# A float32 product with block-diagonal weights, issued as four 64x64 tiles in place of two 128x128 products

## The chip, the cores and the metric

The kernel runs on one core of a Trainium2 chip. The metric is the device time of one launch in microseconds (us); several launches are timed and the median is taken. One further launch is run under the hardware profiler, and all rows of the trace come from that launch. The engines appear under the profile's names: PE is the matrix engine, PEld its weight loads (shown apart, since they overlap the products), DVE, ACT and POOL the vector, scalar and general engines, SP the engine that issues most of the DMAs.

## The reference

The layer is one block of a streaming encoder. One input projection feeds two kinds of heads, 16 of forgetting attention and 32 of a gated delta-rule recurrence (RWKV-7); their gated outputs go through an output projection, a residual sum and a LayerNorm.

```python
proj = jnp.einsum('bsd,dc->bsc', x, w_in)            # 256 x 4096 by 4096 x 16592
fox_out = _fox_attention(fq, fk, fv, log_f)          # 16 heads of 128
y = _rwkv7_scan(rh, decay, kh, vh, -kk, kk * ah)     # 32 heads of 64
...
def frame_step(state, inp):                          # once per frame and head
    r_t, w_t, k_t, v_t, a_t, b_t = inp
    sa = jnp.einsum('bhvk,bhk->bhv', state, a_t)
    state = (state * w_t[:, :, None, :] + sa[..., None] * b_t[:, :, None, :]
             + v_t[..., None] * k_t[:, :, None, :])
    return state, jnp.einsum('bhvk,bhk->bhv', state, r_t)
...
h = jnp.concatenate([fox_out, rwkv_out], axis=-1) * jax.nn.silu(z)
out = jnp.einsum('bsc,cd->bsd', h, w_out)            # 256 x 4096 by 4096 x 4096
x = _layernorm(ALPHA * x + out, ln_gain, ln_bias, LN_EPS)
```

The recurrence is not run frame by frame. The 256 frames are cut into four chunks of 64, and inside a chunk the term `sa` of all 64 frames is the solution of a triangular system: a residual `R` (64 frames by 64 values for each head) is multiplied by the inverse of a 64x64 unit-triangular matrix of that head. This product is what is changed.

## The kernel before, in words

**Main stream.** PE runs the input projection in 32 blocks (eight column groups `n`, four blocks `b` each; function `block`) and then the output projection (`project`). Each weight tile arrives by DMA as float32 and is split by `split` into a high part (ACT, line 141) and a low part (DVE, line 142) in the rounded float32 type, so that each product is made of three: lines 147, 148 and 149 for the input projection (tiles called `acc`), lines 882, 883 and 884 for the output projection (tiles called `oacc`). Each of these has 128x128 weights and 512 moving columns.

**Side work.** The recurrence, the attention, the transposes and the gates are Python generators that `slot()` advances by one step after every second group of three main products; each `yield` in them is one step further down the main stream. So the small products of the recurrence sit inside the main stream on PE, in an order that the number of `yield`s asks for and that the framework's scheduler then fixes when the program is built. Semaphore waits keep every engine in its own order.

**The recurrence.** `rwkv(n)` handles a group of four heads: index `u` (two) times index `j` (two). The two heads `j` of one `u` share the 128 partitions: head `j=0` lies on partitions 0 to 63, head `j=1` on 64 to 127; `HALF` names these two slices. `X` (128 partitions, 2, 4 chunks, 128 columns) holds the inverses; it is set to zero once at the start, and afterwards only the two 64x64 diagonal blocks are written (lines 633 and 667), so each 128x128 slab `X[:, u, c, :]` is block-diagonal. For each chunk `c` the steps on PE are:

- `rh` (line 648): the residual, two float32 products with 128x128 weights; DVE and ACT copy its two halves into `R` (line 651)
- `up` (line 679): the inverse times `R`, two float32 products, `X[:, u, c, :]` against `R[:, u, :]` with 64 moving columns; ACT and DVE copy its two halves into `UV` (line 682)
- `sp` (line 689): the state for the next chunk, not after the last chunk

After the fourth chunk `yp` (lines 709 and 711) makes the outputs. Ahead of the chunks stand `gp` (line 534: the products of keys and queries), `qt` (line 639) and `xp` (line 663: the off-diagonal 32x32 block of each inverse). Four of these already use a part of PE's array: `gp` has weights of 64 partitions by 128 columns, `yp` of 128 partitions by 64 columns, `qt` and `xp` of 32 by 32.

In the trace every float32 product shows as two weight loads and two matmul records: 2 products by 4 chunks by 8 groups at line 679 are 128 of each.

Of the kernel before, what the change touches and what calls it, by code (L numbers as in the profile page):

```python
# [22 lines left out]
C = 64  # L23
# [61 lines left out]
def layer(ctx: ExitStack, tc: tile.TileContext, xt, xtok, w_main, w_lora, w_first, muv, w_o, up, par, mulora, fbias, lng, lnb, cst, out):  # L85
    nc = tc.nc
# [8 lines left out]
    def pst(name):  # L95
        return ps.tile([P, 512], F32, tag="ps", name=name)
# [93 lines left out]
    def wait(n):  # L190
        for _ in range(n):
            yield
# [69 lines left out]
    X = rp.tile([P, 2, NCH, P], F32, name="X")  # L262
# [129 lines left out]
    HALF = [slice(0, C), slice(C, P)]  # L392
# [4 lines left out]
    def flat(t):  # L397
        return t.rearrange("p a b -> p (a b)")
# [121 lines left out]
    def rwkv(n):  # L520
# [8 lines left out]
        for u in range(2):  # L529
            for c in range(NCH):  # L530
                for j in range(2):
                    h = HALF[j]
# [15 lines left out]
        for u in range(2):  # L548
            for j in range(2):
                h = HALF[j]  # L550
# [68 lines left out]
        for j in range(2):  # L619
            o = HALF[1 - j]  # L620
            for c in range(2):
                h = HALF[c]
# [22 lines left out]
        def residual(c):  # L645
            rh = pst(f"rh{n}_{c}")
            for u in range(2):
                nc.tensor.matmul(rh[:, u * P : (u + 1) * P], LT[:, u, c, 0:P], flat(SVt[:, u, c]), start=True, stop=True)  # L648
            R = rp.tile([P, 2, C], F32, tag="R", name=f"R{n}_{c}", bufs=2)
            for j in range(2):  # L650
                (nc.scalar.copy if j else nc.vector.tensor_copy)(R[HALF[j]], diagonal(rh, j))
            return R

        def diagonal(t, j):
            return t[HALF[j], : 2 * P].rearrange("p (u j t) -> p u j t", u=2, j=2)[:, :, j]
# [13 lines left out]
        R = residual(0)  # L669
        yield  # L670

        for c in range(NCH):
            if c:
                R = residual(c)
                yield
            yield
            upp = pst(f"up{n}_{c}")
            for u in range(2):
                nc.tensor.matmul(upp[:, u * C : (u + 1) * C], X[:, u, c, :], R[:, u, :], start=True, stop=True)  # L679
            uv = upp[:, : 2 * C].rearrange("p (u t) -> p u t", u=2)  # L680
            for j in range(2):
                (nc.vector.tensor_copy if j else nc.scalar.copy)(UV[j][HALF[j], :, c, :], uv[HALF[j]])
            yield
            if c == NCH - 1:
                break
            yield
            sp = pst(f"sp{n}_{c}")
            for u in range(2):
                nc.tensor.matmul(sp[:, u * P : (u + 1) * P], BKt[:, u, c, :], flat(UVt[:, u, c]), start=True, stop=True)  # L689
            for j in range(2):  # L690
                h = HALF[j]
                if c == 0:
                    nc.vector.tensor_copy(SV[j][h, :, 1, :], diagonal(sp, j))
                else:
                    nc.vector.tensor_tensor(SV[j][h, :, c + 1, :], diagonal(sp, j), sl[h], ALU.add)
            if c < NCH - 2:
                sl = rp.tile([P, 2, C], F32, tag="sl", name=f"sl{n}_{c}")
                for j in range(2):
                    for u in range(2):
                        nc.scalar.mul(sl[HALF[j], u], SV[j][HALF[j], u, c + 1, :], lc[HALF[j], u, c + 1 : c + 2])  # L700
            yield from wait(2)
# [78 lines left out]
    def chain():  # L780
        while not ff:
            yield
        yield from forget()
        for n in range(G // 2):
            yield from rwkv(n)
# [352 lines left out]
```

## Time and profile before

| | |
|---|---|
| median of three timed launches | 1917.26 us (1916.16 to 1917.36) |
| the profiled launch, its own time | 1917.13 us |
| span in the profile, first to last instruction | 1915.3 us |
| PE busy | 1903.0 us, 9784 products |
| PEld busy | 1584.8 us, 9784 loads |
| DVE busy | 1398.3 us |
| ACT busy | 985.9 us |
| POOL busy | 261.5 us |
| DMA, mean | 220 GB/s |

The span runs from the first to the last instruction; the time of the launch is 1.8 us longer. Products are pipelined on PE: the record of one overlaps the next, and its length contains the time until its last result is written. What a product costs the main stream is therefore read from the distances between starts, not from the lengths of records. In the rows of the timeline the columns are start and length in us, engine, line, operation, output<-inputs, weights (partitions*columns), moving operand and type; `x4` means that four records in a row are merged into one. A note in square brackets gives idle time ahead of the row and what ended it.

### The profile page before, as it was taken

The page shows a single profiled execution, that of the slowest core. Times are in us where ns is not written, and L with a number is a line of the kernel's source. Part 1 is how long each engine was busy: PE and PEld are TensorE (multiplying, and loading weights), DVE is VectorE, ACT ScalarE, POOL GpSimd, SP SyncE. Part 2 cuts the span into 40 slices and gives each one's busy share as a digit, 9 for nine tenths or more (in the row PEclk, how much of TensorE's full clock was granted, in tenths as well). Part 3 has the DMA queues.
Part 4 walks back from the last instruction along what each step waited for, and adds up shares of the span by engine and source line. Part 5 has one row for each costly group of instructions (what it writes and reads, how often), then busy time and mean ns, then how long its engine had stood idle before and what let it go on. Part 6 is the DMA issues. An engine that isn't in the chain of part 4 may idle for free.

```text
span 1915.3 us, 27998 instructions
## 1 busy us (share of the span) xinstructions
PE 1903.0 (99%) x9784; PEld 1584.8 (83%) x9784; DVE 1398.3 (73%) x2359; ACT 985.9 (51%) x1543; POOL 261.5 (14%) x463
## 2 busy tenths in 40 slices
PE   9999999999999999999999999999999999999998
PEld 9878888888888888888888888888888878888886
DVE  6677868786877687768776877787778865765555
ACT  6554565455545654465446554645464554444332
POOL 0022102110211021102200220022002201000000
PEclk9999999999999999999999999999999999999999
DMA  9578767876787677767876687668767976876664
GB/s 338 152 232 230 205 198 235 229 216 190 228 232 220 189 228 224 230 191 217 233 227 193 208 242 226 194 208 246 215 196 207 300 255 199 271 222 202 183 203 170
DMA packets 269682, 420.58 MB, mean 220 GB/s; under 512 B 142370, under 2 KB 169396, under 8 KB 269540
## 3 DMA queue, kind: packets, MB, share of 16 engines
q1 hardware_dynamic: 269108, 418.10, 72.8%
q8 instruction: 77, 1.26, 0.3%
q10 hardware_dynamic: 432, 0.69, 0.1%
q14 instruction: 65, 0.53, 0.1%
HBM read 389.07 MB, written 29.64 MB: 219 GB/s over the span
## 4 chain that ended last, share of the span: by engine, by line
PE 97%; DVE 1%; ACT 0%; issue 0%; DMA 0%; DVEq 0%; ACTq 0%
PE acc L147 24%; PE acc L149 24%; PE acc L148 24%; PE oacc L884 6%; PE oacc L882 6%; PE oacc L883 6%; PE rh L648 1%; PE gp L534 1%; PE up L679 1%; PE sp L689 1%; PE accl L147 1%; PE accl L148 1%; PE accl L149 1%; PE yp L711 0%; PE yp L709 0%; PE fsp L746 0%
## 5 line engine op out<-in xcount | busy, mean ns | idle before, releaser
L761 POOL COPY pT<-lg 32x96 f32<-32x96 f32 x128 | 58.5, 457 | 641.7 <-DVE lg L757 636.9
L604 DVE TENSOR_REDUCE xc<-prod 128x8 f32<-128x16 f32 (+30 forms) x248 | 72.7, 293 | 6.5
L571 POOL COPY BKt<-BK 32x192 f32<-32x192 f32 x128 | 68.6, 536 | 58.6 <-DVE BK L568 53.6
L601 DVE TENSOR_TENSOR prod<-Nb,xc 128x8 f32<-128x8 f32 (+30 forms) x248 | 72.2, 291 | 3.0
L142 DVE TENSOR_TENSOR w_0l<-w,w_0h 128x1024 fp32r<-128x1024 f32 x31 | 38.7, 1248 | 38.2 <-ACT w_0h L141 25.0
L141 ACT CAST w_0h<-w 128x1024 fp32r<-128x1024 f32 x31 | 32.5, 1048 | 51.5 <-DMA w<-in_w_main_dram 31.0
L142 DVE TENSOR_TENSOR w_11l<-w,w_11h 128x1024 fp32r<-128x1024 f32 x31 | 37.9, 1224 | 23.3 <-PE acc L149 17.7
L142 DVE TENSOR_TENSOR w_9l<-w,w_9h 128x1024 fp32r<-128x1024 f32 x31 | 38.0, 1225 | 21.6 <-issue 8.0
L142 DVE TENSOR_TENSOR w_10l<-w,w_10h 128x1024 fp32r<-128x1024 f32 x31 | 38.0, 1224 | 20.6 <-ACT w_10h L141 8.0
L142 DVE TENSOR_TENSOR w_15l<-w,w_15h 128x1024 fp32r<-128x1024 f32 x31 | 38.0, 1226 | 19.4 <-issue 15.9
L141 ACT CAST w_8h<-w 128x1024 fp32r<-128x1024 f32 x31 | 32.6, 1052 | 37.6 <-DMA w<-in_w_main_dram 12.5
L141 ACT CAST w_1h<-w 128x1024 fp32r<-128x1024 f32 x31 | 32.7, 1054 | 34.8 <-DMA w<-in_w_main_dram 18.9
L142 DVE TENSOR_TENSOR w_6l<-w,w_6h 128x1024 fp32r<-128x1024 f32 x31 | 37.9, 1221 | 17.3 <-ACT hry L722 10.3
L147 PE MATMUL acc<-w_15h,x 128*128 128x512 f32 x124 | 50.2, 405 | 0.0
L147 PE MATMUL acc<-w_9h,x 128*128 128x512 f32 x124 | 50.0, 403 | 0.0
L141 ACT CAST w_6h<-w 128x1024 fp32r<-128x1024 f32 x31 | 32.6, 1053 | 33.0 <-PE acc L148 23.0
L147 PE MATMUL acc<-w_14h,x 128*128 128x512 f32 x124 | 49.5, 399 | 0.0
L141 ACT CAST w_13h<-w 128x1024 fp32r<-128x1024 f32 x31 | 32.5, 1050 | 32.6 <-PE acc L148 31.9
L147 PE MATMUL acc<-w_1h,x 128*128 128x512 f32 x124 | 49.1, 396 | 0.0
L147 PE MATMUL acc<-w_2h,x 128*128 128x512 f32 x124 | 49.1, 396 | 0.0
L147 PE MATMUL acc<-w_0h,x 128*128 128x512 f32 x124 | 49.1, 396 | 0.0
L147 PE MATMUL acc<-w_5h,x 128*128 128x512 f32 x124 | 49.1, 396 | 0.0
(818 smaller groups left out, 6633.7 us busy)
## 6 DMA issues: line engine op xcount, KB each, us to landing
w<-in_w_main_dram SPq DMA_DIRECT2D x496, 512.0 KB, 4.1
wo<-in_w_o_dram SPq DMA_DIRECT2D x128, 512.0 KB, 4.1
bt<-bk SPq DMA_DIRECT2D x88, 128.0 KB, 4.2
Nb<-nd SPq DMA_DIRECT2D x16, 512.0 KB, 4.6
hd<-hl SPq DMA_DIRECT2D x29, 256.0 KB, 2.2
h<-hd SPq DMA_DIRECT2D x29, 256.0 KB, 6.1
wr<-in_w_first_dram SPq DMA_DIRECT2D x15, 384.0 KB, 6.1
lr<-in_w_lora_dram SPq DMA_DIRECT2D x14, 336.0 KB, 6.5
```

What stands on the lines that cost most here:

```text
L141: nc.scalar.copy(hi[:, :n], src[:, :n])
L142: latest[0] = nc.vector.tensor_tensor(lo[:, :n], src[:, :n], hi[:, :n].bitcast(F32), ALU.subtract)
L147: nc.tensor.matmul(acc[:, :n], xs[k][:, 0, tt], hi[:, o : o + n], start=(k == 0), stop=False)
L148: nc.tensor.matmul(acc[:, :n], xs[k][:, 1, tt], hi[:, o : o + n], start=False, stop=False)
L149: nc.tensor.matmul(acc[:, :n], xs[k][:, 0, tt], lo[:, o : o + n], start=False, stop=(k == KT - 1))
L571: nc.gpsimd.tensor_copy(BKt[B * b : B * (b + 1), :, :, B * a : B * (a + 1)], BK[B * a : B * (a + 1), :, : NCH - 1, B * b : B * (b + 1)])
L601: first = nc.vector.tensor_tensor(prod[:, :, :, s + 1 :], nb[:, :, s : s + 1, s + 1 :].to_broadcast([P, 2, NJ, w]), xc[:, :, :, s + 1 :], ...
L604: solved = nc.vector.tensor_reduce(xc[:, :, :, s : s + 1], prod[:, :, :, s:], AX.X, ALU.add)
L761: (nc.gpsimd.tensor_copy if b % 2 else nc.scalar.copy)(pT[B * b : B * (b + 1), :, B * a : B * (a + 1)], lg[B * a : B * (a + 1), :, B * b : ...
L882: nc.tensor.matmul(acc, ht[k][:, 0, tt], hi, start=(k == 0), stop=False)
L883: nc.tensor.matmul(acc, ht[k][:, 1, tt], hi, start=False, stop=False)
L884: nc.tensor.matmul(acc, ht[k][:, 0, tt], lo, start=False, stop=(k == KT - 1))
```

## The change

The weights of a product are now one diagonal 64x64 block of `X`, and the moving operand and the output are the matching half of the partitions. The two off-diagonal blocks, which are zero, are no longer multiplied. What is computed is the same.

```diff
             upp = pst(f"up{n}_{c}")
             for u in range(2):
-                nc.tensor.matmul(upp[:, u * C : (u + 1) * C], X[:, u, c, :], R[:, u, :], start=True, stop=True)
+                for h in HALF:
+                    nc.tensor.matmul(upp[h, u * C : (u + 1) * C], X[h, u, c, h], R[h, u, :], start=True, stop=True)
             uv = upp[:, : 2 * C].rearrange("p (u t) -> p u t", u=2)
```

All lines behind line 678 have a number one higher in the changed kernel, so `up` is line 680 there. On DVE, ACT, POOL and SP the order of the built program is unchanged. On PE, in 30 of the 32 chunks, the four products stand where the two stood. An example is the first chunk of group `n=0`, where the main stream is at block `b=0` of the next group (the lines with - and + are before and after; the last two numbers are the moving operand's partitions and columns, and the other numbers only tell tiles apart):

```order
 L148 MATMUL acc_0_1_2187<-w_0_8h,x_513 128x512
 L149 MATMUL acc_0_1_2187<-w_0_8l,x_513 128x512
-L679 MATMUL up_0_2407<-R_0_2384,X 128x64 x2
+L680 MATMUL up_0_2407<-R_0_2384,X 64x64 x4
 L147 MATMUL acc_0_0_2186<-w_0_8h,x_516 128x512
 L148 MATMUL acc_0_0_2186<-w_0_8h,x_516 128x512
```

Nothing around it has moved.

In two chunks the scheduler puts the first of the four earlier than the other three. The first place is the third chunk of the first group, on PE:

```order
 L147 MATMUL acc_0_0_2186<-w_0_14h,x_744 128x512
 L148 MATMUL acc_0_0_2186<-w_0_14h,x_744 128x512
+L680 MATMUL up_2_2590<-R_2_2569,X 64x64
 L149 MATMUL acc_0_0_2186<-w_0_14l,x_744 128x512
+L680 MATMUL up_2_2590<-R_2_2569,X 64x64 x3
 L147 MATMUL acc_0_1_2187<-w_0_14h,x_744 128x512
-L679 MATMUL up_2_2586<-R_2_2565,X 128x64 x2
 L148 MATMUL acc_0_1_2187<-w_0_14h,x_744 128x512
 L149 MATMUL acc_0_1_2187<-w_0_14l,x_744 128x512
```

The products `up` stand one main product earlier, and one main product stands between the first and the other three. In the next chunk of the same group `rh` also moves one main product ahead.

The second place is the first chunk of the last group, where the output projection already runs. PE before, with the engines that each product waits for:

```order
L882 MATMUL oacc_0_14964<-wo_8h,h_14895 128x512
L883 MATMUL oacc_0_14964<-wo_8h,h_14895 128x512
L884 MATMUL oacc_0_14964<-wo_8l,h_14895 128x512
L679 MATMUL up_0_15258<-R_0_15219,X 128x64 [waits PE_49,Activation_49]
L679 MATMUL up_0_15258<-R_0_15219,X 128x64
L882 MATMUL oacc_1_14965<-wo_8h,h_14895 128x512
L883 MATMUL oacc_1_14965<-wo_8h,h_14895 128x512
```

and now:

```order
L883 MATMUL oacc_0_15020<-wo_8h,h_14951 128x512
L884 MATMUL oacc_0_15020<-wo_8h,h_14951 128x512
L680 MATMUL up_0_15314<-R_0_15275,X 64x64 [waits DVE_49,Activation_49]
L885 MATMUL oacc_0_15020<-wo_8l,h_14951 128x512
L680 MATMUL up_0_15314<-R_0_15275,X 64x64 [waits Activation_49]
L680 MATMUL up_0_15314<-R_0_15275,X 64x64 x2
L883 MATMUL oacc_1_15021<-wo_8h,h_14951 128x512
```

Again one of the four has gone ahead of a main product. The wait has become finer: a product of the lower half waits for DVE's copy of `R`, one of the upper half for ACT's, where before the first of the two products waited for the later copy, which is ACT's.

## The prediction

> **What bounds the kernel now.** I read the page first: the share of each engine, the granted clock, and the chain that ended last.
>
> ```profile
> PE 1903.0 (99%) x9784; PEld 1584.8 (83%) x9784; DVE 1398.3 (73%) x2359; ACT 985.9 (51%) x1543; POOL 261.5 (14%) x463
> PEclk9999999999999999999999999999999999999999
> PE 97%; DVE 1%; ACT 0%; issue 0%; DMA 0%; DVEq 0%; ACTq 0%
> ```
>
> PE is on the chain for 97% of the span, at full clock in every slice. So whatever a small product takes of PE's stream lengthens or shortens the launch by as much, unless PE waits for somebody close behind it. The view of waits, taken for PE from 100 to 1600 us, has only these two:
>
> ```profile
> PE acc L149 <- DVE w_10l L142: 1.0, 1, 1.0
> PE sp L689 <- DVE UV L682: 0.3, 1, 0.3
> ```
>
> The first `up` is at 235 us. The timeline has the first of these waits near 102 us, ahead of it, and the second near 1571 us, so at most 0.3 us of added PE work can vanish in a wait.
>
> What one `up` takes of the stream is read from the timeline of PE, around the first chunk of the second group:
>
> ```profile
> 424.61 0.39 PE L148 MATMUL acc<-w_8h,x 128*128 128x512 f32 x1
> 424.83 0.39 PE L149 MATMUL acc<-w_8l,x 128*128 128x512 f32 x1
> 425.06 0.55 PE L679 MATMUL up<-R,X 128*128 128x64 f32 x4
> 425.42 0.48 PE L147 MATMUL acc<-w_8h,x 128*128 128x512 f32 x1
> 425.74 0.39 PE L148 MATMUL acc<-w_8h,x 128*128 128x512 f32 x1
> 424.84 0.64 PEld L679 LDWEIGHTS up<-R,X 128*128 128x128 f32 x4
> ```
>
> Main products start 0.22 to 0.23 us apart. From the main product ahead of `up` (424.83) to the second one behind it (425.74) are 0.91 us; without `up` it would be 2 x 0.23 = 0.46. So `up` costs 0.45 us, 32 times, 14.4 us in all. The last row shows why it isn't more: its first weight load starts at 424.84, while the main product is still running, so it enters with no gap. The four records themselves are paced by their loads of 128 columns.
>
> **The change part by part.** Removed are four full-array records per chunk; added are eight records with 64x64 weights, on two tiles that don't share partitions. No such record is in the trace, but four uses of a part of the array are, and all are unlike `up` at their edges. `yp` has 64 columns of weights and 64 moving columns, as the new products have, and 128 partitions in place of 64:
>
> ```profile
> 456.15 0.40 PE L149 MATMUL acc<-w_1l,x 128*128 128x512 f32 x1
> 456.48 0.34 PE L711 MATMUL yp<-lt,SV 128*64 128x64 f32 x4
> 456.65 0.29 PE L709 MATMUL yp<-gb,UV 128*64 128x64 f32 x4
> 456.76 0.29 PE L711 MATMUL yp<-lt,SV 128*64 128x64 f32 x4
> ...
> 458.16 0.29 PE L711 MATMUL yp<-lt,SV 128*64 128x64 f32 x4
> 458.28 0.29 PE L709 MATMUL yp<-gb,UV 128*64 128x64 f32 x4
> 458.50 0.50 PE L147 MATMUL acc<-w_2h,x 128*128 128x512 f32 x1
> 458.83 0.39 PE L148 MATMUL acc<-w_2h,x 128*128 128x512 f32 x1
> 456.48 0.20 PEld L711 LDWEIGHTS yp<-lt,SV 128*64 128x64 f32 x4 [0.36 <-PE acc L148]
> ```
>
> Entry: the first record starts 0.33 us behind the main product's start, not 0.23, and its load has not been made ahead: PEld stands idle for 0.36 us. Exit: the first main product behind starts 0.22 us after the last group of four, but the second only 0.34 us later (458.50 to 458.83), so a main product's load and the end of the tiles lie bare. In the middle a group of four records takes 0.117 us (456.76 to 458.16 are twelve groups, 1.40 us), the first 0.17.
>
> The other ends are the two uses with 32 and with 128 columns:
>
> ```profile
> 415.91 0.39 PE L149 MATMUL acc<-w_5l,x 128*128 128x512 f32 x1
> 416.22 0.69 PE L639 MATMUL qt<-T,gb 32*32 32x32 f32 x32
> 416.85 0.50 PE L147 MATMUL acc<-w_6h,x 128*128 128x512 f32 x1
> 417.19 0.40 PE L148 MATMUL acc<-w_6h,x 128*128 128x512 f32 x1
> 416.22 0.58 PEld L639 LDWEIGHTS qt<-T,gb 32*32 32x32 f32 x32 [0.35 <-issue]
> 334.81 0.39 PE L149 MATMUL acc<-w_9l,x 128*128 128x512 f32 x1
> 335.12 2.06 PE L534 MATMUL gp<-lt,BK 64*128 64x128 f32 x32
> 337.11 0.50 PE L147 MATMUL acc<-w_9h,x 128*128 128x512 f32 x1
> 337.45 0.39 PE L148 MATMUL acc<-w_9h,x 128*128 128x512 f32 x1
> L639 PE MATMUL qt<-T,gb 32*32 32x32 f32 x256 | 5.5, 192 | 0.0
> L534 PE MATMUL gp<-lt,BK 64*128 64x128 f32 x256 | 16.4, 278 | 0.0
> ```
>
> Entry is 0.31 us in both, exit is the same 0.34. So the bare entry and exit don't depend on the tile's form, only the middle does. The last two rows group all records and give their mean length, 192 and 278 ns, which is the tail behind the last start. `qt` so starts 32 records in 0.69 - 0.19 = 0.50 us, 0.016 each; `yp` needs 0.029, `gp` 2.06 - 0.28 = 1.78, 0.056 each. This goes with the columns, 32, 64, 128, and not with the partitions, 32, 128, 64. All three alternate between two tiles, as the new loop over `h` does.
>
> Cost of a chunk's `up` after the change, from the main product ahead to the second one behind: by `yp`, 0.33 + 0.17 (first four records) + 0.55 (start of the last four to the second main product, 458.28 to 458.83) = 1.05; with the entry of `qt` and `gp` 1.03. I take 1.04 against 0.91, a loss of 0.13 to 0.14. By `qt`: 1.28 for 32 records less 24 x 0.016 = 0.90, no change. By `gp`: 2.64 less 24 x 0.056 = 1.30, a loss of 0.39. I take `yp`, which has the same columns of both operands.
>
> [...]
>
> **The two divided chunks.** In the third chunk of the first group and the first chunk of the last, one main product stands between the first new product and the other three. Entry and exit come twice there. What of 1.04 us is not records or main products is 1.04 - 0.23 (eight records at 0.029) - 0.46 = 0.35; records that have no partner on the other tile, and the slower first four, add some 0.1. So 0.45 more each, 0.9 together.
>
> [...] Two chunks pay a wait for ACT's copy of `R` now:
>
> ```profile
> 264.50 0.39 PE L149 MATMUL acc<-w_1l,x 128*128 128x512 f32 x1
> 265.54 0.39 PE L148 MATMUL acc<-w_1h,x 128*128 128x512 f32 x1
> 1567.26 0.39 PE L884 MATMUL oacc<-wo_8l,h 128*128 128x512 f32 x1
> 1568.28 0.40 PE L883 MATMUL oacc<-wo_8h,h 128*128 128x512 f32 x1
> 1567.49 0.52 PEld L679 LDWEIGHTS up<-R,X 128*128 128x128 f32 x4 [0.27 <-ACT R L651]
> ```
>
> They take 1.04 and 1.02 us instead of 0.91. The new products enter later anyway, and in the second place the first one needs DVE's half alone. So 0.13 + 0.11 = 0.24 us go.
>
> **The readers at no cost.** ACT waits longest for `up` at its copies, and queued behind them are the casts of the weights that PE needs:
>
> ```profile
> ACT UV L682 <- PE up L679: 30.3, 21, 2.6
> ```
>
> The last record of `up` ends at 425.06 + 0.55 = 425.61, 0.78 us behind the main product's start. With tiles it is 0.33 + 0.17 + 0.29 = 0.79. So the copies start as they did, measured against PE, and what is late behind is PE itself. If they came 0.1 us later, the main stream's three tiles in hand would cover it. DMA, DVE and POOL only gain time.
>
> **Sum.** 32 x 0.135 = 4.3; plus 0.9; less 0.24: 5.0 us. The profiled launch took 1917.13 us, 0.13 under the median. 1917.13 + 5.0 = 1922.1, slower by 0.26%.
>
> **The rivals.** About 0.2%, 3.8 us here, is what a measurement of this kernel can tell from no change.
>
> - *The eight records are as cheap as 32x32 ones.* By `qt`: 32 x -0.01 + 0.9 - 0.24 gives +0.3 and 1917.5. For it: the tiles are diagonal, as `qt`'s are. Against it: 64 columns cost `yp` nearly twice what 32 cost `qt`. Anything between, up to 0.12 us a chunk, also counts as no change. 0.16.
> - [...] If the load of the next tile went ahead as `up`'s does now, the burst would be eight records at 0.029, 0.23 us, in place of 0.45: 32 x 0.22 = 7.0 us faster, 1910.1. It decides if the idle time of PEld at the entry is under 0.1 us. Against it: `gp`, `qt` and `yp` all show the late entry. 0.08.
> - *The two halves don't run side by side.* Then the eight loads of 64 columns follow one another at 0.058: 0.23 us more a chunk, 1.27 in all, 32 x 0.36 + 0.7 = 12.2 us slower, 1929.3. Against it: `gp` (two row halves) and `yp` (two column halves) both overlap; no trace shows halves of both at once with 64. 0.08.
> - *The mechanism that I forecast*, 0.68, itself from 1921.2 (1.03 a chunk, the divided chunks at half price) to 1922.9 (1.05 a chunk, 0.6 for each divided one, no wait hidden).
>
> The first of these also stands for the change not doing what it says: less array, yet the same time.
>
> [...]
>
> **How the numbers follow.** Slower by over 0.2%: nearly all of 0.68 (0.66) and the third rival's 0.08, 0.74. Within 0.2%: 0.16 and 0.02 of the forecast, 0.18. Faster: 0.08. The range begins at 1917.5, the price by `qt`; the price by `gp`, 32 x 0.39 + 0.7 = 13.1 us, would end it at 1930.3, but only the third rival lies there, so it ends at 1926, where half of the records fail to overlap. The two outer rivals, 0.16 in all, are left out.
>
> **What would show it.** Loads of `up` start some 0.32 us behind the main product with PEld idle before them; eight records follow in two tiles, last start about 0.23 us after the first; the second main product behind starts 0.33 to 0.34 after the first. From the product ahead to the second behind are 1.03 to 1.05 us in 30 chunks, and PE's busy time hardly rises, since a gap hides in the record ahead. I am wrong if this distance is 0.91 or less, if it is 1.2 or more, or if it is 1.04 and the span has not grown by 4 to 6 us, because something behind PE absorbed it.

## The result, and the profile after

Six launches of each kernel: 1917.72 us before (1916.16 to 1920.49) and 1925.97 us after (1923.24 to 1928.33). The ratio is 1.0045, its 95% interval 1.0035 to 1.0054: slower by 8.3 us where 5.0 were forecast. The profiled launch took 1927.53 us with a span of 1925.7, so it lies 1.6 us above the median; the rows of this section are its own.

First the shares on the page of the kernel after, the chain's shares by engine (fourth row), and the row of queue 8, which is explained further down:

```profile
span 1925.7 us, 28261 instructions
PE 1907.8 (99%) x9912; PEld 1576.0 (82%) x9912; DVE 1397.4 (73%) x2359; ACT 985.2 (51%) x1543; POOL 263.1 (14%) x463
q8 instruction: 78, 1.28, 0.3%
PE 94%; DVE 3%; DMA 1%; issue 1%; ACT 0%; SPq 0%; DVEq 0%; ACTq 0%
```

PE is busy for 4.8 us more. But it is also idle for 5.6 us more: 1925.7 less 1907.8 is 17.9, where 1915.3 less 1903.0 was 12.3. So only about half of the loss is work of PE. Its share of the chain fell from 97% to 94%, and DVE and DMA have a larger part in it, 3% and 1% (1% and 0% before). Something ahead of PE has become late.

The price of `up` itself is read as it was before, from the timeline of PE around the first chunk of the second group:

```profile
426.82 0.39 PE L149 MATMUL acc<-w_8l,x 128*128 128x512 f32 x1
427.14 0.45 PE L680 MATMUL up<-R,X 64*64 64x64 f32 x8
427.52 0.50 PE L147 MATMUL acc<-w_8h,x 128*128 128x512 f32 x1
427.86 0.39 PE L148 MATMUL acc<-w_8h,x 128*128 128x512 f32 x1
427.14 0.31 PEld L680 LDWEIGHTS up<-R,X 64*64 64x64 f32 x8 [0.35 <-issue]
```

From 426.82 to 427.86 are 1.04 us, in place of 0.91. The load starts 0.32 us behind the main product, with PEld idle for 0.35 us before it. A divided chunk looks so:

```profile
254.35 0.40 PE L148 MATMUL acc<-w_14h,x 128*128 128x512 f32 x1
254.68 0.33 PE L680 MATMUL up<-R,X 64*64 64x64 f32 x2
254.93 0.49 PE L149 MATMUL acc<-w_14l,x 128*128 128x512 f32 x1
255.35 0.44 PE L680 MATMUL up<-R,X 64*64 64x64 f32 x6
255.73 0.50 PE L147 MATMUL acc<-w_14h,x 128*128 128x512 f32 x1
256.06 0.39 PE L148 MATMUL acc<-w_14h,x 128*128 128x512 f32 x1
```

That is 1.71 us; less the 0.23 of the main product in the middle and the 1.04 of an ordinary chunk, 0.44 are left, against 0.45 in the forecast. The new products cost what was said.

What was not said stands in the view of PE's waits, again from 100 to 1600 us (total us, times, longest):

```profile
PE acc L149 <- DVE w_5l L142: 5.2, 6, 1.4
PE acc L149 <- DVE w_10l L142: 1.0, 1, 1.0
PE up L680 <- DVE R L651: 0.6, 1, 0.6
```

Six times the main stream waits for the low half of one weight tile, `w_5l`. Measured on the distances between main products (each beyond its usual 0.227 us) these six stalls take 1.59, 0.35, 0.73, 1.30, 0.90 and 1.25 us, 6.1 in all. The whole difference of the two spans, 10.3 us, adds up on PE. I summed the time from each main product to the next one by what lies between them; a distance counts in the second column when `up` lies in it. The two divided chunks put two more distances there (34 in place of 32), so 0.45 us of that column is time of main products, which the column of main products alone lacks.

| after less before, us | first product starts | around `up` | around `sp` | main products alone | span |
|---|---|---|---|---|---|
| the kernel after | -0.36 | +5.49 (0.9 of it the wait for DVE's `R`) | -0.70 | +5.94 | +10.3 |

### The profile page after: what moved, and what is told of

It reads as the page before. It is cut to its first block, busy times and chain, and to the rows that moved or that the text cites. A ratio compares the mean times of both kernels' runs of the same rounds, so it can differ in the third digit from the quotient of the medians.

```text
span 1925.7 us, 28261 instructions
## 1 busy us (share of the span) xinstructions
PE 1907.8 (99%) x9912; PEld 1576.0 (82%) x9912; DVE 1397.4 (73%) x2359; ACT 985.2 (51%) x1543; POOL 263.1 (14%) x463
## 3 DMA queue, kind: packets, MB, share of 16 engines
q8 instruction: 78, 1.28, 0.3%
## 4 chain that ended last, share of the span: by engine, by line
PE 94%; DVE 3%; DMA 1%; issue 1%; ACT 0%; SPq 0%; DVEq 0%; ACTq 0%
PE acc L147 23%; PE acc L149 23%; PE acc L148 23%; PE oacc L883 6%; PE oacc L885 6%; PE oacc L884 6%; PE gp L534 1%; PE rh L648 1%; PE up L680 1%; PE sp L690 1%; PE accl L149 0%; PE accl L148 0%; PE accl L147 0%; PE yp L712 0%; DVE w_5l L142 0%
## 5 line engine op out<-in xcount | busy, mean ns | idle before, releaser
L149 PE MATMUL acc<-w_5l,x 128*128 128x512 f32 x124 | 49.0, 396 | 5.2 <-DVE w_5l L142 5.2
L142 DVE TENSOR_TENSOR w_6l<-w,w_6h 128x1024 fp32r<-128x1024 f32 x31 | 37.9, 1221 | 17.3 <-ACT hry L723 10.3
L147 PE MATMUL acc<-w_11h,x 128*128 128x512 f32 x124 | 49.1, 396 | 0.0
L147 PE MATMUL acc<-w_8h,x 128*128 128x512 f32 x124 | 49.1, 396 | 0.0
```

The source lines that it names most:

```text
L142: latest[0] = nc.vector.tensor_tensor(lo[:, :n], src[:, :n], hi[:, :n].bitcast(F32), ALU.subtract)
L147: nc.tensor.matmul(acc[:, :n], xs[k][:, 0, tt], hi[:, o : o + n], start=(k == 0), stop=False)
L149: nc.tensor.matmul(acc[:, :n], xs[k][:, 0, tt], lo[:, o : o + n], start=False, stop=(k == KT - 1))
```

## What delays w_5l

The chain of waits runs back through three engines. These are rows of the kernel after, at the first of the six stalls, from the timelines of SP, ACT, DVE and PE (start, us, engine, line; in brackets the idle time before and who ended it):

```profile
308.79 0.33 SPq L415 DMA_DIRECT2D upt<-in_up_dram  x1
310.00 0.38 SPq L935 DMA_DIRECT2D vd<-bk  x1
313.90 0.41 ACT L420 CAST uph<-upt 96x256 fp32r<-96x256 f32 x1 [2.11 <-DMA upt<-in_up_dram]
317.41 1.18 DVE L142 TENSOR_TENSOR w_4l<-w,w_4h 128x1024 fp32r<-128x1024 f32 x1
323.78 1.22 DVE L142 TENSOR_TENSOR w_5l<-w,w_5h 128x1024 fp32r<-128x1024 f32 x1
325.06 0.50 PE L149 MATMUL acc<-w_5l,x 128*128 128x512 f32 x1 [1.43 <-DVE w_5l L142]
```

And the same place before:

```profile
308.57 0.33 SPq L415 DMA_DIRECT2D upt<-in_up_dram  x1
309.78 0.38 SPq L934 DMA_DIRECT2D vd<-bk  x1
311.76 0.41 ACT L420 CAST uph<-upt 96x256 fp32r<-96x256 f32 x1 [0.19 <-DMA upt<-in_up_dram]
315.27 1.18 DVE L142 TENSOR_TENSOR w_4l<-w,w_4h 128x1024 fp32r<-128x1024 f32 x1
321.66 1.23 DVE L142 TENSOR_TENSOR w_5l<-w,w_5h 128x1024 fp32r<-128x1024 f32 x1
323.25 0.39 PE L149 MATMUL acc<-w_5l,x 128*128 128x512 f32 x1
```

`upt` is a small load of 96 partitions for the recurrence's next group. It is issued 0.22 us later than before, yet ACT gets it 2.14 us later. ACT stands in its wait, and DVE's `w_4l` and `w_5l`, which need ACT's halves of the same tiles, move back by 2.1 us. Before, `w_5l` was done at 321.66 + 1.23 = 322.89 and PE used it at 323.25: 0.36 us in hand. Neither row is near an `up`.

Why is the load late? The view of the DMA engines for 310 to 314 us (40 slices of 0.1 us, mean busy share in tenths; then packets, MB and share of 16 engines for each queue) shows, for the kernel after:

```profile
DMA  8795449567778999743110000000010000000999
GB/s 369 328 410 215 154 144 318 133 82 205 277 287 307 348 348 358 266 154 113 62 41 20 0 0 0 0 10 10 0 20 0 10 10 10 20 31 20 317 102 266
q1 hardware_dynamic: 447, 0.56, 54.3%
q8 instruction: 1, 0.02, 3.2%
```

From about 312.0 to 313.7 us nearly all DMA engines are idle, though `upt` and `vd` have not landed; what still moves, 0 to 31 GB/s, is a trickle. And there is one packet of the queue called "instruction". 3.2% of 16 engines for 4 us are 2.05 us of one engine.

The packet records show what that packet did. It lasts from 310.63 to 312.68 us. From 312.21 to 312.67 no packet of a load starts. Then they come one behind the other, as of one engine: six of 1 KB and one of 4 bytes, which ends at 313.35, then sixteen of 1 KB and one of 4 bytes, which ends at 314.06. `upt` is 96 rows of 1 KB and `vd` 256, so six and sixteen are a sixteenth of each, the part of one of 16 engines. Behind the first part ACT gets `upt`, at 313.90; behind the second `vd` lands, at 314.51. So the last sixteenth of both loads stood behind the instruction packet.

The page's row for this queue has 78 packets and 1.28 MB, 16.4 KB each; PE and PEld have 2 x 9912 = 19,824 records, 254 to a packet (before: 77 packets, 19,568 records, 254): 256 records more, one packet more. By this count and the queue's name I read the packets as PE's instructions, brought by DMA some 254 records at a time. PE's waits above name no such packet; its cost shows on the two loads that stood behind it.

The change adds four records of PE and four of PEld per chunk, 32 per group of four chunks. Between the first `up` of one group and of the next the trace has 2000 loads and matmuls before and 2032 after: with 254 recorded to a packet, 7.87 and 8.00 packets. After the change a group is a whole number of packets, and the packet falls at nearly the same place in every group. From the packet records, for each group (us):

```
             packet starts, behind       vd landed and    idle of ACT     stall of PE
             the issue of vd; lasts      vs issued after  before uph      at w_5l
after   g1   0.63   2.05                 4.53             2.11            1.59
        g2   0.54   0.98                 3.37             0.95            0.35
        g3   1.15   0.96                 3.97             1.70            0.73
        g4   1.72   1.01                 4.54             2.30            1.30
        g5   0.93   1.48                 4.22             1.86            0.90
        g6   0.86   1.83                 4.50             2.24            1.25
before  g1   0.98   1.75                 4.23             0.19            none
        g2 to g6: no packet from 0 to 5 us behind; vs issued after 2.33 to 3.19, no stall
```

PE's stall follows ACT's wait for `upt` with some 0.5 to 1.0 us taken off, which is what lay in hand. Before, one group of six met a packet, and even there `upt` was hardly touched: the rows left behind the packet are sixteen, those of `vd` alone.

The last group, g7, tells the two loads apart. The last `upt` is issued 23 us ahead of `vd` there, and not 1.2. The packet met `vd` in both kernels (it started 1.02 us behind `vd`, and `vs` was issued after 4.37, in the kernel after; 0.49 and 3.00 before), and PE did not stall.

This is the theory that I tested, called the fetch: the tiles cost what was forecast, and the rest is the place of the instruction packets. Rivals were that the tiles themselves make the main stream wait, wherever the packets lie; that the reading of less array is worth something; and that the two halves don't run side by side.

## The experiments

All kernels compute the whole result. The comparison is always with the kernel before on the same chip.

**1. Move the packets.** Sixteen idle products of 32 columns at the end of the warm-up, 32 records, move every packet by an eighth of its length of program. Nothing else differs from the kernel after.

```diff
+    for n in range(16):
+        nc.tensor.matmul(wps[:, :32], idle[:, :P], idle[:, :32], start=True, stop=True)
```

> The changed kernel with 16 more idle products of 32 columns behind the six warm-up products, 32 PE instructions, so that the 16 KB packets of PE's instruction stream (one for 256 PE instructions) are fetched some 3.4 us earlier in every group. Theory F (the fetch): the packet no longer falls 0.5 to 1.7 us behind the issue of vd, vd lands after 2.5 us again and not 4.2, PE's waits for w_5l (5.2 us in the changed kernel) shrink to under 1 us, and the time is 1922 to 1924 (about 5 us less, plus up to 1 us for the added products at the start). Theory P (the later entry of the tiles shifts PE against DVE and ACT by itself): waits stay near 5 us and the time is 1926 to 1928.

Measured: 1921.71 us (1920.53 to 1923.24), ratio 1.0017, interval 1.0008 to 1.0026. The interval doesn't touch that of the kernel after. In the profiled launch there is no wait for `w_5l`; the packets start 2.0 to 3.8 us ahead of `vd`'s issue or further off. The same window of the DMA engines:

```profile
DMA  9594533127999999997990693142979989595393
q1 hardware_dynamic: 559, 0.95, 81.7%
```

There is no instruction packet in it, and no hole. `vd` (time to landing, from the view of the tile, which dates three of the eight; first the kernel after, then this one) is quick again:

```profile
DMA to landing us min/median/max: 4.0/4.2/4.5
...
DMA to landing us min/median/max: 2.3/2.3/2.7
```

**2 and 3. As many records, without tiles.** The kernel before, with each `up` product split into two of 32 moving columns on the full array. It has the records of the kernel after, and no tiles. Then the same with the sixteen idle products.

```diff
-                nc.tensor.matmul(upp[:, u * C : (u + 1) * C], X[:, u, c, :], R[:, u, :], start=True, stop=True)
+                for g in range(2):
+                    o = u * C + g * B
+                    nc.tensor.matmul(upp[:, o : o + B], X[:, u, c, :], R[:, u, g * B : (g + 1) * B], start=True, stop=True)
```

> The kernel before with each product up split into two of 32 moving columns: eight full-array records a chunk, as many PE instructions per group as in the changed kernel, no tiles. Eight loads of 128 columns at 0.11 us in place of four: 0.45 us more a chunk, 14.3 us in all. Theory F: the fetch stands at the same place in every group, behind the issue of vd; vd lands after some 4.2 us, PE waits 3 to 6 us more for w_5l, time 1935 to 1938. Theory P: without tiles no such waits, time 1931 to 1932.

> The kernel of the split columns with the 16 idle products at the start. Theory F: vd lands after 2.5 us, PE's waits for w_5l under 1 us, time 1931 to 1933, some 4 us under the one without the idle products. Theory P: 0 to 1 us over the one without them.

Measured: 1934.25 us, ratio 1.0083 (1.0069 to 1.0097), and 1930.14 us, ratio 1.0068 (1.0056 to 1.0081). One `up` takes 1.35 us here: less two main products, 0.90 for eight records with weights of 128 columns, where the kernel before has 0.45 for four. A record so costs 0.112 us with 32 moving columns as with 64. In the first, packets start 0.58 to 1.85 us behind `vd` in all seven groups, and PE waits for the same tile; in the second the view has no such wait (the distances show one stall of 0.29 us). Both times lie about 1 us under what was expected. The waits of PE in experiment 2:

```profile
PE acc L149 <- DVE w_5l L142: 3.7, 4, 1.2
```

So the stall needs no tiles: the number of records and the place of the packet make it. The two intervals overlap a little; the waits tell the kernels apart more clearly than the times.

**4. The order of the tiles.** `h` outside, `u` inside, so that two neighbouring products share a tile. One launch.

```diff
-            for u in range(2):
-                for h in HALF:
+            for h in HALF:
+                for u in range(2):
```

> The changed kernel with the loops over h and u exchanged, so that two products stand on one tile and then two on the other. If the two tiles run side by side whatever the order in the program, the distance from the main product ahead to the second behind stays 1.03 to 1.05 us. If they overlap only when they alternate, it rises to 1.15 to 1.27 us.

Measured: 1927.7 us; one `up` takes 1.042 us in place of 1.035, where the rival had 1.27. The halves run side by side in either order. The rival that they don't has nothing for it. PE waits for `w_5l` here too, 3.9 us.

**5. A whole packet of idle products.** 128 in place of 16 should bring the packet back to where it was.

> The changed kernel with 128 idle products at the start in place of 16: 256 PE instructions, one whole packet, so every later instruction stands at the same place within its packet as in the changed kernel. 16 of them took 0.5 us, so 128 take some 4 us, of which 3.5 delay the first product. Theory F: the fetch stands behind vd again, vd lands after 3.5 to 4.7 us, PE waits 4 to 7 us for w_5l, time 1928 to 1931. Rival S (any added products at the start help, through the warmer start or the later one): no such waits, time 1924 to 1925.5.

Measured: 1924.67 us (1923.30 to 1927.64), ratio 1.0039 (1.0023 to 1.0054). The packet did come back, 0.35 to 0.93 us behind `vd`'s issue in all seven groups, and `vd` is slow again:

```profile
DMA to landing us min/median/max: 3.2/3.4/3.6
PE acc L151 <- DVE w_5l L144: 0.2, 1, 0.2
```

But `upt` was hardly late (1.8 us in 5 waits), and PE waited 0.2 us for `w_5l`, where I had expected 4 to 7. The time went to the start instead: the 128 idle products take 3.6 us, and the first main product starts 2.5 us later than before. PE also waits 1.4 us once for `wo_7h` in the output projection, which the kernel before doesn't; the cause is open. The profiled launch is the fastest of the four, 1923.30 us, so the others may have met more. The place in time of the packet is thus not all that decides. The packet records show the difference: in g4 and g5 the rows left behind the instruction packet are sixteen, those of `vd` alone, where the kernel after has 22, `upt`'s six too, in g1 and g3. Why `upt`'s rows were through here when the packet started, 2.0 to 2.1 us behind `upt`'s issue, and not there at 1.8 and 2.4, is open.

**6. The idle products without the tiles.** The sixteen idle products on the kernel before.

> The kernel before with the 16 idle products at the start. Theory F: the fetch drifts against the groups here, so it meets vd in one or two groups whatever the start, with no wait of PE behind it; time within 1 us of before. Rival S: the idle products by themselves are worth several us, and this is 3 us or more faster than before, 1915 or less.

Measured: 1918.05 us, ratio 1.0000 (0.9991 to 1.0009). So the idle products cost nothing that can be told, and the difference of experiments 1 and 6, 3.7 us, is an estimate of the price of the tiles without the collision. It may be low, since 6 has a collision of its own. In two groups a packet now starts 2.3 and 2.1 us behind `vd`, and in the first of these the untiled kernel shows the whole chain, where I had expected no wait of PE:

```profile
PE acc L151 <- DVE w_5l L144: 1.6, 1, 1.6
```

**7. Tiles in three chunks of four.** The last chunk of each group stays on the full array: 24 records more a group in place of 32, so the packet should drift.

```diff
+                if c == NCH - 1:
+                    nc.tensor.matmul(upp[:, u * C : (u + 1) * C], X[:, u, c, :], R[:, u, :], start=True, stop=True)
+                    continue
```

> The changed kernel with the last chunk of each group as before: 24 tiled chunks and 8 full ones, 8 PE instructions fewer in a group, so the fetch comes some 0.9 us later in each group and meets vd in the first two or three alone. The tiles cost 24 x 0.13 = 3.1, divided chunks 0.9. Theory F: waits for w_5l 1 to 3 us in all, in the early groups, time 1922 to 1924. Theory P, waits in proportion to the tiled chunks: three quarters of the changed kernel's loss, in all groups, 1924 to 1925.

Measured: 1921.56 us (1920.35 to 1923.52), ratio 1.0020 (1.0011 to 1.0028). The packet starts 0.88, 1.34, 0.77, 2.03, 4.21, 5.03 and 6.93 us behind `vd`: it drifts out of the way. PE stalls in the first two groups (and by 0.16 us, in the distances, in the third):

```profile
PE acc L149 <- DVE w_5l L142: 1.9, 2, 1.0
```

**8. Columns alone.** Two tiles of 128 partitions by 64 columns.

```diff
-                    nc.tensor.matmul(upp[h, u * C : (u + 1) * C], X[h, u, c, h], R[h, u, :], start=True, stop=True)
+                    nc.tensor.matmul(upp[h, u * C : (u + 1) * C], X[:, u, c, h], R[:, u, :], start=True, stop=True)
```

> The changed kernel with weights of 128 partitions by 64 columns, the zero block included: the tiles are halved by columns alone. If columns set the pace and any change of the tile's form drains, the distance from the main product ahead to the second behind stays 1.03 to 1.05 us. If halving the partitions was worth something, it is longer, 1.1 or more; if it cost something, shorter, 1.0 or less.

Measured, one launch: 1927.5 us, with PE's wait for `w_5l` as in the kernel after (first row). Its timeline at the same chunk:

```profile
PE acc L149 <- DVE w_5l L142: 5.2, 6, 1.2
...
426.00 0.39 PE L149 MATMUL acc<-w_8l,x 128*128 128x512 f32 x1
426.32 0.45 PE L680 MATMUL up<-R,X 128*64 128x64 f32 x8
426.70 0.50 PE L147 MATMUL acc<-w_8h,x 128*128 128x512 f32 x1
427.04 0.39 PE L148 MATMUL acc<-w_8h,x 128*128 128x512 f32 x1
```

It is the burst of the 64x64 tiles to the hundredth, 1.04 us. By "drains" the expectation means the idle time of PEld ahead of a burst, 0.35 us in the kernel after. Leaving out the zero half of the partitions bought nothing; the columns and the edges set the price.

**9 and 10. Load `upt` one group ahead.** If the stall goes through `upt`, an early load ends it, whatever the packet does to `vd`. Done on the kernel after and, for the edit's own price, on the kernel before.

```diff
-            ups[i] = rp.tile([LORA, 2, P], F32, tag="upt", name=f"upt{i}")
+            ups[i] = rp.tile([LORA, 2, P], F32, tag="upt", name=f"upt{i}", bufs=2)
...
-        load_up(i + 1)
+        load_up(i + 2)
...
+    load_up(1)
```

> The changed kernel with two buffers for the small weights upt and each loaded one front earlier, so that nobody waits for this load when the fetch of PE's instructions delays it; the fetch and vd stay where they are. If the way from the fetch to PE goes through upt (ACT's cast of it, ACT's queue behind it, DVE, w_5l): ACT's wait for upt (9.5 us in the changed kernel) and PE's waits for w_5l (5.2 us) both go to under 1 us, while vd still lands after 3.5 us or more; time 1921 to 1923. If it goes through vd and the loads queued behind it on SP: PE's waits stay at 3 us or more and the time at 1925 to 1928.

> The kernel before with the same two buffers and earlier loads. It has no wait of PE for w_5l in its profile and 1.3 us of ACT's waits for upt, so within 1 us of before; if launches in which the fetch meets upt are what spreads its times from 1915.6 to 1922.4, the median falls by up to 1 us and the spread narrows.

Measured: 1925.29 us, ratio 1.0039 (1.0025 to 1.0054), and 1921.18 us, ratio 1.0017 (1.0008 to 1.0026). The wait for `w_5l` is gone from the first, though `vs` is still issued only 3.0 to 4.0 us behind `vd`. So in this launch the path is through `upt`. It is the fastest of the five (1923.23 us), and the median is no lower than that of the kernel after in experiment 11, so the times don't show it. But the edit costs 3.3 us by itself, where I had put it within 1 us of nothing: ACT's cast no longer waits for the load but for PE's `lp`, which reads the tile that it writes, and by the distances between main products PE stalls seven times by 0.26 to 0.38 us at a later tile, `w_13l`, with the edit in both kernels. ACT's and PE's waits in experiment 9:

```profile
ACT uph L420 <- DMA upt<-in_up_dram: 0.3, 1, 0.3
ACT uph L420 <- PE lp L429: 24.6, 10, 6.0
...
PE acc L149 <- DVE w_13l L142: 0.4, 2, 0.2
```

The price of the tiles, taken between these two kernels, is 4.1 us.

The other twelve traces bear out the path. They have 72 groups g1 to g6. In 30 of these ACT stood idle for 0.95 us or more ahead of the cast of `upt`, and all 30 have a stall at `w_5l` by the distances, 0.16 to 1.76 us; of the other 42 one has (0.38 us, in experiment 5). A packet started 0 to 2.5 us behind `vd` in 41 of the 72, and 11 of these have no stall. So it takes a late `upt`, and a packet beside `vd` does not always make one.

**11. The kernel after once more.**

> The changed kernel again, for how far its profile repeats. Theory F: the fetch stands 0.5 to 1.7 us behind vd in groups two to eight again and PE waits for w_5l 3 to 6 us; time 1924 to 1928.

Measured: 1924.98 us (1922.29 to 1928.48), ratio 1.0035 (1.0021 to 1.0050). In its profiled launch, 1928.48 us and the slowest of the five, the packet lies 1.77 us ahead of `vd` in the first group, with no stall there, and 0.8 to 2.4 us behind it in the others; the stalls come in five groups. The interval overlaps that of experiment 1 by a little; the single launches (1920.53 to 1923.24 there) and the wait tell the two apart:

```profile
PE acc L149 <- DVE w_5l L142: 5.6, 5, 1.6
```

**12. Half a packet.** 64 idle products put the packet as far from `vd` as it can be.

> The changed kernel with 64 idle products at the start, half a packet, where 16 took the waits away and 128 (a whole packet) brought a part of them back. They take some 2 us, of which 1.4 delay the first product. Theory F: the fetch is half a packet's time from vd, no packet within 3 us of its issue, vd lands after 2.3 to 2.7 us, PE's waits for w_5l under 0.5 us, time 1921.5 to 1923.5, under the one with 128. Rival S (more idle products at the start cost time by themselves, in proportion): between the 1921.7 of 16 and the 1924.7 of 128, near 1923, with some of the waits for w_5l.

Measured: 1920.92 us (1920.31 to 1921.47), ratio 1.0014 (1.0005 to 1.0023). No packet lies within 6 us of `vd`, and PE doesn't wait for `w_5l`. The eleven launches lie within 1.2 us of each other, those of the kernel after within 5 to 6. A collision that comes out differently each time would do this, but that was not traced launch by launch, and the launches of the kernel before, with no stall at `w_5l` in its trace, spread by 3.8 to 6.5 us as well.

The sum on PE for four of these profiled launches, against the kernel before, as in the table above:

| after less before, us | first product starts | around `up` | around `sp` | main products alone | span |
|---|---|---|---|---|---|
| 1, sixteen idle products | -0.40 | +4.59 | -0.71 | -0.16 | +3.7 |
| 12, sixty-four | +0.84 | +4.58 | -0.71 | -1.47 | +3.2 |
| 5, a hundred and twenty-eight | +2.52 | +4.97 | -0.69 | -0.71 | +6.1 |
| 11, the kernel after again | -0.29 | +5.10 | -0.70 | +7.29 | +11.4 |

What is missing to the span lies at other bursts, at most 0.4 us. The column of `up` is the same in all but for the wait for DVE's `R` (0.4 us in 5, 0.5 in 11, none in 1 and 12). Why the column of the main products is 1.3 us lower in 12 than in 1 isn't known. What sets the kernel after apart is the column of the main products. No kernel here beats the one before.

## Why the prediction was right and where it was wrong

**Direction: right.** Slower, and for the reason given as one part of it.

**The burst: right.** 1.04 us was the forecast from `yp`, 1.035 the median. The entry of 0.32 us, the idle 0.35 of PEld, the 0.34 to the second main product came as the neighbouring bursts had them. What is neither records nor main products, 1.04 less 0.23 and 0.46, was the same 0.35 us a burst whether the tiles are cut in columns (experiment 8) or in both ways. Why PEld stands idle at the entry, no run shows. By experiment 2 a full-array record costs 0.112 us (1.353 less 0.906, over four), so the burst of before was four records, 0.45 us, with nothing for its edges; the new one is eight at `yp`'s 0.029, 0.23 us, and the 0.35.

Two readings beside it were wrong. The 0.34 us to the second main product is hardly a mark of tiles: `up` before has 0.32 there (425.42 to 425.74). And PE's busy time was to hardly rise, since a gap hides in the record ahead; it rose by 4.8 us, because a gap that hides in a record counts as busy (the record ahead of the burst above ends at 426.82 + 0.39 = 427.21, behind the start at 427.14).

**The divided chunks: right,** 0.44 more each for 0.45.

**The waits hidden: right, but too few.** The two waits for ACT's `R` went, 0.24 us. Around `sp` another 0.70 went: the `sp` behind each divided chunk had waited for `UV` (0.80 and 1.21 us from main product to main product in place of 0.59). In experiment 8, where no chunk is divided, the second of these is still there, 1.19 us; with the division it is 0.73. So more than the 0.3 us could vanish that the prediction read from PE's waits; the view of the tile had `PEld sp L689: 0.8, 1`. In the profiled launch a wait of 0.9 us for DVE's `R` came in at the first `up`; in experiments 1 and 12 it isn't there. Its cause is open.

**The sum without the collision.** 5.0 was forecast. Read from the distances in experiment 1, its own terms come to 4.8: 32 x 0.129 = 4.1, 0.9 for the divided chunks, less 0.24. Less 0.7 at `sp` and 0.4 at the start, 3.7 are left; the start is chance, since the first main product starts at 4.35 to 4.76 us in the nine traces without added idle products. Experiments 1 against 6 gave 3.7, 9 against 10 gave 4.1, and experiment 12 2.7 by its medians (1920.92 less 1918.24). So this sum was too high by some 1 to 2 us, of which 0.7 is the gain at `sp`.

**The step that failed: "The readers at no cost".** It said that "DMA, DVE and POOL only gain time", and that "the main stream's three tiles in hand would cover it". In its place the runs showed a wait of 5 to 6 us for `w_5l` in both profiled launches of the kernel after, in no term of the sum. It had two errors. The step followed only who reads `up`, while the 256 records more on PE were themselves a change on the DMA engines: one packet more, and the others at other places. And the cover was stated as three tiles at all places, while the trace of before shows 0.36 us in hand at `w_5l` in the first group (321.66 + 1.23 against 323.25). Both were to be seen before: 77 packets for 19,568 records, a packet in the first group beside a `vd` behind which SP could go on after 4.2 us where the next five took 2.3 to 3.2, and 32 records more to 2000, which makes eight packets of 254. That the collision would also reach `upt` could not be read there, since in that one group it didn't.

**The range and the rivals.** The median lies at the very end of the range, and outside of the 1921.2 to 1922.9 that the likeliest case gave itself (its terms give 1922.8). That it isn't past 1926 is luck: that end stood for halves that fail to overlap, and the burst of 1.035 us shows none of that. The prediction's own sign of being wrong, 1.04 us and a span that has not grown by 4 to 6, came: it grew by 10.3. But nothing behind PE absorbed the burst's price, as that sign had it; a wait was added. None of the rivals is what happened: 32x32 prices, no late entry, and halves one after the other all speak of the burst, and the burst was not where the miss was. A chunk's `up` went from 0.45 to 0.58 us net of two main products.

**What is settled.** That the place of the instruction packets makes the extra wait: moving them by idle products alone takes it away (1, 12), records without tiles bring it (2), and idle products without tiles bring one of it to the kernel before (6). That it goes through `upt`: in the traces the stall comes with ACT's wait for `upt`, and where `upt` is early, in g7 and in experiment 9, it is absent while `vd` stays late. Open is why the packet finds `upt`'s rows still waiting in some groups and not in others, those of experiment 5 above all; and how often the launches that weren't traced stall.

## What to carry to other kernels

The burst of small tiled products paid some 0.35 us for its edges inside this full-array stream, so it had to save more than that in its middle; eight records of 64 columns in place of four of 128 saved 0.22 us (0.45 to 0.23). Where an edit brings a loop's records on PE near a whole number of packets (here 2032 a group, 8.00 packets of 254), look in the trace at which small loads the instruction packets meet, and move them with a few idle products before judging an edit of a few us. And read the time in hand at each tile from the trace, at the tightest place of the loop, rather than from the number of buffers.

## What the runs showed of the hardware

- A packet of instructions took 0.9 to 2.05 us, and the 256 KB transfer that it met landed 1 to 2 us later (`vd`: 4.0 to 4.5 us in the kernel after, 2.3 to 2.7 in experiment 1). At the first stall a sixteenth of two loads, 22 rows of 1 KB, went on only when the packet had ended, at 312.67 us.
- Sixteen 32-column products, which cost nothing measurable in themselves (1.0000, interval 0.9991 to 1.0009), moved the time of the changed kernel from 1.0045 to 1.0017.
- Halving the partitions of a 64-column tile changed nothing: 1.035 us a chunk with 128x64 and with 64x64 tiles.
